# Cached attention's steps counted at every half-tile with other rates by section, and a fifth raw weight tile in the first phase of a hybrid decoder layer

## The chip, the core and the metric

The kernel runs on one core of a Trainium2 chip. The metric is the device time of one execution in microseconds (us). A core has five engines with instruction queues of their own: TensorE (PE in the profile, with its weight loads as PEld), VectorE (DVE), ScalarE (ACT), GpSimd (POOL) and SyncE (SP). Each runs its queue in order and waits on semaphores; SP, ACT and POOL also issue DMAs.

## What is computed

One layer of a decoder, for 512 prompt rows and 8 sequences of 8 sample rows, in float32:

```
h = rms_norm(x) @ w_in                       # -> q, k, v (8 heads of 128), forget gate, conv value and gate
attn  = softmax attention with cumulative log-forget bias
        prompt: 4 query blocks of 128 per head, causal
        sample: 8 queries per sequence over 2048 cached keys (16 pages of 128) and the 8 new ones
conv  = GLU -> causal depthwise conv of width 31 -> LayerNorm over channels -> swish
x = x + concat(rms_norm(attn), conv) @ w_out
x = x + relu(rms_norm(x) @ w_up)**2 @ w_down
x = x + (p @ w_ple) * sigmoid(rms_norm(x) @ w_ple_gate);   y = rms_norm(x)
```

The cache holds keys and values of 8 sequences x 16 pages x 8 heads, 128 MiB in all, fetched page by page through a page table.

## The kernel before

All 576 rows stand in the free dimension, as two halves of 288. Every float32 product is made as three matmuls on split operands: a high part (ACT copies, `whi`) and a low part (DVE subtracts, `wlo`).

**Phase 1** makes the input projection, both attentions, the convolution and the operands of the output projection. Its projection runs tile by tile: one tile is 128 output columns over 16 blocks of the contraction, cut into four chunks; `gemm_tile` (L506) yields after each half chunk. Such a *half-tile* is 12 pairs of (weight block, part) products, 24 matmuls written as L497. At each yield `half()` (L364) runs a little of the other work: steps of the convolution (`side`), of the prompt's heads (`att`), and of the cached attention (`D["dec"]`).

The weights of phase 1 come through `WStream` (L100). `high(c)` issues on ACT's queue the load of chunk c+3 into a tile `wraw`, then copies chunk c to `whi`; `low()` lets DVE subtract it to `wlo`. `get` prepares two chunks ahead. There are 4 `wraw` tiles and 3 of `whi` and `wlo` each.

The cached attention is the generator `decode` (L836): 68 steps, after a first call that only starts loads. A step n below 64 makes the scores of four pages of keys for four heads (L864); a step from 4 on makes the product of weights and values (L895) of the step four before. At every fourth step the scores' maximum is taken on DVE into the tile `dp`, and at the next the exponentials are transposed on PE (L854) through the PSUM buffer T, which the prompt's heads use as well (L749, L782, L805); ACT copies them out (L856). `kv_load` (L820) issues the loads on SP's queue: two key tiles and two value tiles for each step, each tile as two DMAs of 256 KB. Keys have 5 tiles, values 4, in two pools: `deca` (three of each, and `dp`) and `decb` (the others). A step's last call of `kv_load` comes after its matmuls, so SP waits there for the tiles that they release.

When a step runs is set by a credit: on every second half-tile `half()` adds `D["rate"]`, and at 1 it runs one step and takes 1 away. The rate comes from `DEC_RATE` by the number of the entry in `order` (L266): 11 entries (c0, q4 to c5; six convolution entries of 16 half-tiles and five others of 8), then 5 (v0, c6, k1, c7, v1), then 12 (the keys and values of heads 2 to 7). They have 136, 56 and 96 half-tiles, and are called sections 1, 2 and 3 here. In section 3 the convolution's normalisation and the prompt's heads run beside.

When the decoder is exhausted, its pools are closed and `mid` is opened for what leads to the output projection. **Phase 2** (from about 840 us) holds the output projection, MLP and gate, and is not touched.

Of the kernel before, what the change touches and what calls it, by code (L numbers as in the profile page):

```python
# [9 lines left out]
F32 = mybir.dt.float32  # L10
# [15 lines left out]
EPS = 1e-6  # L26
SCALE = 128.0 ** -0.5
NEG = -1.0e30
DEC_RATE = (11, 0.43), (16, 0.47), (99, 0.61)
DOWN_FIRST = (3, 3, 3, 4, 5, 6, 7, 8)  # L30
DOWN_PART = 7
RING = 8
# [67 lines left out]
class WStream:  # L100


    AHEAD, RAW = 2, 4

    def __init__(self, nc, pool, srcs):
        self.nc, self.pool, self.srcs = nc, pool, srcs
# [1 line left out]

    def dma(self, n):
        while self.sent < min(n, len(self.srcs)):  # L110
            t = self.pool.tile([128, 4, 128], F32, name="wraw", tag="wraw", bufs=self.RAW)
            (self.nc.sync if self.sent < self.RAW else self.nc.scalar).dma_start(t, self.srcs[self.sent])
            self.raw[self.sent] = t
            self.sent += 1
# [28 lines left out]
class Kern:  # L143
# [99 lines left out]
    def phase1(self):  # L243
# [15 lines left out]
        O_ = lambda: po_.tile([128, 512], F32, name="O", tag="O")  # L259
        D_ = lambda: pd_.tile([128, 512], F32, name="D", tag="D")  # L260
        U_ = lambda: pu.tile([128, 2, 512], F32, name="U", tag="U")
# [88 lines left out]


        side, att, fq = deque(), deque(), deque()
        D = {"credit": 0.0, "half": 0, "dec": None, "mid": None, "rate": 0.0}

        def step(q):
            while q:
                try:
                    next(q[0])
                    return True
                except StopIteration:  # L360
                    q.popleft()
            return False

        def half():  # L364

            D["half"] += 1
            odd = D["half"] % 2
            self.flush_later()
            if D["dec"] is None:
                step(att)  # L370
                step(fq)
                return
            step(side)
            step(att)
            if odd:
                return
            D["credit"] += D["rate"]
            if D["credit"] >= 1.0:
                D["credit"] -= 1.0
                if next(D["dec"], self) is self and D["mid"] is None:  # L380
                    des.close()
                    D["mid"] = mes.enter_context(tc.tile_pool(name="mid", bufs=2, reuse_waits="tile"))
                    self.ple_loads(D["mid"])
                    side.append(self.finish(1, D_, O_))

        def run(gen):
            for _ in gen:
                half()
# [41 lines left out]
        dec = D["dec"] = self.decode()  # L430
        next(dec)

        for n, (kind, i) in enumerate(order):
            D["rate"] = next(r for m, r in DEC_RATE if n < m)
            if kind == "c":
# [10 lines left out]
            if kind == "q":  # L446
                t = hd.tile([128, NR], F32, name="q", tag="q", bufs=2)
# [388 lines left out]
    def decode(self):  # L836


        nc, sm = self.nc, self.sm
        V = nc.vector.tensor_tensor  # L840
        tiles, load = self.kv, self.kv_load
        s = o = mu = p = None
        al, ls = {}, {}
        one = lambda name: sm.tile([128, 1], F32, name=name, tag=name)
        for n in range(68):
            if n == 0:
                load(0, 5)
                yield
            sc, w = n // 4, n % 4
            G, c = sc // 4, sc % 4  # L850
            if n >= 4 and w == 0:
                t = self.T_()
                for i in range(4):
                    nc.tensor.transpose(t[:, i * 128:i * 128 + 128], p[:, i * 128:i * 128 + 128], self.ident)  # L854
                for i, m in ((0, 128), (128, 512)):
                    nc.scalar.activation(self.PT[:, i:m], t[:, i:m], AF.Copy)  # L856
            if n < 64:
                if w == 0:
                    s = self.D_()
                    nc.tensor.matmul(s, self.selU[:, G, :], self.R[:, c * 512:c * 512 + 512], start=True, stop=False)  # L860
                for i in range(2):
                    kt = tiles[0][2 * n + i]
                    for h in range(4):
                        nc.tensor.matmul(s[32 * h:32 * h + 32, i * 256:i * 256 + 256].rearrange("p (a b) -> p a b", a=2),  # L864
                                         self.q_of(G // 2 * 4 + h, G % 2 * 4 + w), kt[:, :, h, :],
                                         start=False, stop=(w == 3 and i == 1))
                if w == 3:
                    p = self.kvp[0].tile([128, 512], F32, name="dp", tag="dp")
                    mx = one("dmx")
                    nc.vector.tensor_scalar(p, s, self.cns[:, G:G + 1], None, ALU.add, ALU.max, accum_out=mx)  # L870
                    new = self.mlu[:, 0, G:G + 1]
                    if c == 0:
                        nc.vector.tensor_copy(new, mx)
                        ls[sc] = self.mlu[:, 1, G:G + 1]
                    else:
                        al[sc], ls[sc] = one("dal"), one("dls")
                        V(mx, mx, new, ALU.max)
                        V(al[sc], new, mx, ALU.subtract)
                        nc.vector.tensor_copy(new, mx)
                    nm = one("dnm")  # L880
                    nc.vector.tensor_scalar(nm, mx, -1.0, None, ALU.mult)

                    def late(p=p, nm=nm, l=ls[sc], d=al.get(sc)):
                        nc.scalar.activation(p, p, AF.Exp, bias=nm, accum_out=l)
                        if d is not None:
                            nc.scalar.activation(d, d, AF.Exp)
                    self.later.append(late)
                load(0, 2 * n + 6)
            if n >= 4:
                m = n - 4  # L890
                if w == 0:
                    o = self.O_()
                for r in range(4):
                    for h in range(4):
                        nc.tensor.matmul(o[32 * h:32 * h + 32, r * 128:r * 128 + 128], self.PT[:, w * 128 + h * 32:w * 128 + h * 32 + 32],  # L895
                                         tiles[1][2 * m + r // 2][:, r % 2, h, :], start=(w == 0 and r == 0), stop=(w == 3 and r == 3))
                if w == 3:
                    self.merge(m // 16, m // 4 % 4, o, al.pop(m // 4, None), ls.pop(m // 4))
            load(1, 2 * n - 2)
            load(0, 2 * n + 7)  # L900
            yield
# [997 lines left out]
```

## Time and profile before

| | us |
|---|---|
| median of 3 runs | 2740.95 (2735.22 to 2743.04) |
| the profiled execution's own time | 2746.47 |
| span in that profile, first to last instruction | 2744.7 |
| PE busy | 2670.7 |
| DVE busy | 2043.5 |
| ACT busy | 1152.6 |
| POOL busy | 511.0 |

A span is read as PE's busy time, its idle time and what a lower granted clock adds. A view by windows gives for each stretch the busy time of each engine with the number of instructions, then the granted PE clock (1.00 is full), the mean busy share of the 16 DMA engines and the GB/s that they moved. A row of the waits has what waited, what ended the wait, us in total, times and the longest. In the timeline, `x16` counts instructions merged into one row, and a bracket gives the idle time ahead of it and what ended it; one float32 matmul of the program (L864, L895) is two of the profile.

### The profile page before, as it was taken

The page shows a single profiled execution, that of the slowest core. Times are in us where ns is not written, and L with a number is a line of the kernel's source. Part 1 is how long each engine was busy: PE and PEld are TensorE (multiplying, and loading weights), DVE is VectorE, ACT ScalarE, POOL GpSimd, SP SyncE. Part 2 cuts the span into 40 slices and gives each one's busy share as a digit, 9 for nine tenths or more (in the row PEclk, how much of TensorE's full clock was granted, in tenths as well). Part 3 has the DMA queues.
Part 4 walks back from the last instruction along what each step waited for, and adds up shares of the span by engine and source line. Part 5 has one row for each costly group of instructions (what it writes and reads, how often), then busy time and mean ns, then how long its engine had stood idle before and what let it go on. Part 6 is the DMA issues. An engine that isn't in the chain of part 4 may idle for free.

```text
span 2744.7 us, 56305 instructions
## 1 busy us (share of the span) xinstructions
PE 2670.7 (97%) x21873; PEld 2575.1 (94%) x21873; DVE 2043.5 (74%) x3553; ACT 1152.6 (42%) x1692; POOL 511.0 (19%) x906
## 2 busy tenths in 40 slices
PE   8999999998999999999999999999999999998997
PEld 8999999877889998999999999999999999998997
DVE  5577777645444447888888888898888888887676
ACT  4222232334443224444444444444444444444554
POOL 2188787601000000000000000100000000000110
PEclk9999999999999999999999999999999999999999
DMA  5488888898754454444444444666565656655675
GB/s 197 148 299 289 301 291 290 287 320 285 253 191 151 160 197 156 154 143 138 138 138 140 145 143 138 242 149 172 164 191 149 182 158 173 179 169 179 199 241 175
DMA packets 238382, 536.12 MB, mean 195 GB/s; under 512 B 25537, under 2 KB 26562, under 8 KB 238114
## 3 DMA queue, kind: packets, MB, share of 16 engines
q1 hardware_dynamic: 170978, 327.86, 37.7%
q0 software_dynamic: 33600, 143.70, 16.7%
q10 hardware_dynamic: 33536, 60.96, 6.9%
q8 instruction: 171, 2.80, 0.4%
q14 instruction: 97, 0.79, 0.1%
HBM read 441.47 MB, written 90.96 MB: 194 GB/s over the span
## 4 chain that ended last, share of the span: by engine, by line
PE 49%; issue 5%; DVE 3%; DMA 1%; ACT 1%; POOL 0%; DVEq 0%; ACTq 0%; POOLq 0%
PE P L1548 14%; PE P L1547 14%; PE P L1549 14%; PE P L1615 2%; PE P L1617 2%; PE P L1616 2%; DVE w2l L152 1%; DMA xs<-x 1%; ACT w2h L149 0%; DMA xs<-di 0%; DMA x<-c 0%; DVE w2r L1770 0%; DVE w2r L1771 0%; DVE w2r L1772 0%; DVE xs L1486 0%
## 5 line engine op out<-in xcount | busy, mean ns | idle before, releaser
L1547 PE MATMUL P<-xs,w2h 128*128 128x288 f32 x3584 | 1064.5, 297 | 17.0 <-DVE c L1664 8.0
L1548 PE MATMUL P<-xs,w2h 128*128 128x288 f32 x3584 | 1064.4, 297 | 4.7 <-DVE xs L152 4.7
L1549 PE MATMUL P<-xs,w2l 128*128 128x288 f32 x3584 | 1061.4, 296 | 2.8 <-DVE w2l L152 2.6
L149 ACT ACTIVATE w2h<-w2r 128x896 fp32r<-128x896 f32 (+1 forms) x632 | 556.0, 889 | 723.7 <-PE P L1548 425.6
L152 DVE TENSOR_TENSOR w2l<-w2r,w2h 128x896 fp32r<-128x896 f32 (+1 forms) x632 | 637.9, 1012 | 218.1 <-ACT w2h L149 215.6
L1547 PEld LDWEIGHTS P<-xs,w2h 128*128 128x128 f32 x3584 | 676.8, 189 | 23.6 <-DVE c L1664 11.1
L1548 PEld LDWEIGHTS P<-xs,w2h 128*128 128x128 f32 x3584 | 677.3, 189 | 7.3 <-DVE xs L152 7.0
L1549 PEld LDWEIGHTS P<-xs,w2l 128*128 128x128 f32 x3584 | 674.9, 188 | 5.1 <-DVE w2l L152 4.9
L497 PE MATMUL U<-xh,whi 128*128 128x288 f32 x1792 | 400.6, 305 | 3.6 <-ACT xh L149 2.2
L497 PE MATMUL U<-xh,wlo 128*128 128x288 f32 x1792 | 385.3, 297 | 1.4 <-DVE wlo L129 1.4
L497 PE MATMUL U<-xl,whi 128*128 128x288 f32 x1792 | 385.2, 297 | 1.6 <-DVE xl L331 1.6
L497 PEld LDWEIGHTS U<-xh,whi 128*128 128x128 f32 x1792 | 288.2, 190 | 22.5 <-issue 16.3
L123 ACT ACTIVATE whi<-wraw 128x512 fp32r<-128x512 f32 x224 | 141.2, 630 | 393.5 <-PE U L497 217.7
L497 PEld LDWEIGHTS U<-xl,whi 128*128 128x128 f32 x1792 | 289.8, 190 | 2.6 <-DVE xl L331 2.5
L497 PEld LDWEIGHTS U<-xh,wlo 128*128 128x128 f32 x1792 | 289.7, 190 | 2.2 <-DVE wlo L129 2.1
L129 DVE TENSOR_TENSOR wlo<-wraw,whi 128x512 fp32r<-128x512 f32 x224 | 160.2, 715 | 133.9 <-ACT whi L123 132.5
L1044 DVE SCALAR_TENSOR_TENSOR y<-ue,cv,y 128x512 f32<-128x512 f32 x240 | 183.8, 766 | 5.3
L1770 DVE TENSOR_TENSOR w2r<-w2r 128x512 f32<-128x512 f32 (+1 forms) x273 | 177.7, 651 | 5.2 <-DMA w2r<-in_w_down 5.2
L1045 POOL TENSOR_SCALAR cvt<-us,cv 128x64 f32<-128x64 f32 x240 | 162.8, 678 | 22.3
L1615 PE MATMUL P<-xs,w2h 128*128 128x288 f32 x512 | 151.8, 297 | 0.4 <-ACT c L1663 0.4
L1617 PE MATMUL P<-xs,w2l 128*128 128x288 f32 x512 | 151.0, 295 | 1.1 <-DVE w2l L152 1.0
L1616 PE MATMUL P<-xs,w2h 128*128 128x288 f32 x512 | 150.8, 295 | 0.0
(382 smaller groups left out, 2761.1 us busy)
## 6 DMA issues: line engine op xcount, KB each, us to landing
k<-in_cache_kv SPq DMA_DIRECT2D x256, 256.0 KB, 4.7
v<-in_cache_kv SPq DMA_DIRECT2D x256, 256.0 KB, 4.6
w2r<-in_w_up SPq DMA_DIRECT2D x127, 512.0 KB, 4.0
w2r<-in_w_down SPq DMA_DIRECT2D x112, 512.0 KB, 4.3
wraw<-in_w_main ACTq DMA_DIRECT2D x156, 256.0 KB, 4.9
xs<-di POOLq DMA_DIRECT2D x32, 1008.0 KB, 6.1
w2r<-in_w_gate SPq DMA_DIRECT2D x60, 512.0 KB, 4.6
x<-c POOLq DMA_DIRECT2D x48, 576.0 KB, 6.4
```

The lines of the kernel that those rows point to most:

```text
L149: self.nc.scalar.activation(out, in_, AF.Copy, **kw)
L152: self.nc.vector.tensor_tensor(out, in_, f(hi), ALU.subtract)
L497: self.nc.tensor.matmul(u[:, r, :HR], w, x[:, r * HR:(r + 1) * HR], start=first and n == 0, stop=last and n == 2)
L1044: nc.vector.scalar_tensor_tensor(y, ue[:, j:j + NPR], w, y, ALU.mult, ALU.add)
L1045: nc.gpsimd.tensor_scalar(t, us[:, :, j:j + 8], w, None, ALU.mult)
L1547: nc.tensor.matmul(o, hi[:, ia, :], s.hi[:, ib, :], start=(i == 0), stop=False)
L1548: nc.tensor.matmul(o, hi[:, ia, :], s.lo[:, ib, :], start=False, stop=False)
L1549: nc.tensor.matmul(o, lo[:, ia, :], s.hi[:, ib, :], start=False, stop=(i == n - 1))
L1615: nc.tensor.matmul(o, hi[:, ia, :], s.hi[:, kh, rows], start=first and kh == 0, stop=False)
L1616: nc.tensor.matmul(o, hi[:, ia, :], s.lo[:, kh, rows], start=False, stop=False)
L1617: nc.tensor.matmul(o, lo[:, ia, :], s.hi[:, kh, rows], start=False, stop=last and kh == 1)
L1770: lambda: V(w[:, :, 4:6, :], w[:, :, 0:1, :].broadcast_to([128, m, 2, 128]), w[:, :, 1:3, :], ALU.add),
```

## The change

Three things are changed.

1. The credit is added at every half-tile instead of every second one, and the rates are 0.2275, 0.245 and 0.2775 for each half-tile instead of 0.43, 0.47 and 0.61 for each two.
2. There are five `wraw` tiles instead of four. The first four loads still go to SP's queue and the prefetch distance stays.
3. The tile `dp` is taken from the pool `decb` instead of `deca`.

```diff
-DEC_RATE = (11, 0.43), (16, 0.47), (99, 0.61)
+DEC_RATE = (11, 0.2275), (16, 0.245), (99, 0.2775)
...
-    AHEAD, RAW = 2, 4
+    AHEAD, RAW, TILES = 2, 4, 5
...
-            t = self.pool.tile([128, 4, 128], F32, name="wraw", tag="wraw", bufs=self.RAW)
+            t = self.pool.tile([128, 4, 128], F32, name="wraw", tag="wraw", bufs=self.TILES)
...
-        D = {"credit": 0.0, "half": 0, "dec": None, "mid": None, "rate": 0.0}
+        D = {"credit": 0.0, "dec": None, "mid": None, "rate": 0.0}
...
         def half():
 
-            D["half"] += 1
-            odd = D["half"] % 2
             self.flush_later()
...
             step(side)
             step(att)
-            if odd:
-                return
             D["credit"] += D["rate"]
             if D["credit"] >= 1.0:
                 D["credit"] -= 1.0
...
-                    p = self.kvp[0].tile([128, 512], F32, name="dp", tag="dp")
+                    p = self.kvp[1].tile([128, 512], F32, name="dp", tag="dp")
```

The edits take four lines out of the file, so a line number of the changed kernel is lower by 4 from L377 on.

How far apart steps 56 to 60 stand follows from the rates. Before, they run at half-tiles 240, 244, 248, 250 and 254 of the 288; after, at 237, 241, 244, 248 and 251. Step 59 on PE: here is the way from step 58 (its L864 and L895) to it before. `xh` and `xl` are the activations' parts, numbered by block; each left-out stretch is the rest of a half-tile.

```order
L864 MATMUL D<-k,q_s 32x256 x8
L895 MATMUL O<-v,PT 32x128 x16
L497 MATMUL U<-xh_191,whi 128x288 x2
...
L757 MATMUL S<-vn,pT 128x128 x3
L497 MATMUL U<-xh_193,whi 128x288 x2
...
L864 MATMUL D<-k,q_s 32x256 x8
L895 MATMUL O<-v,PT 32x128 x16
```

And the same way after:

```order
L860 MATMUL D<-k,q_s 32x256 x8
L891 MATMUL O<-v,PT 32x128 x16
L493 MATMUL U<-xh_199,whi 128x288 x2
...
L753 MATMUL S<-vn,pT 128x128
L493 MATMUL U<-xh_201,whi 128x288 x2
...
L745 MATMUL T<-ident,p 128x128 x3
L730 MATMUL S<-cb,sel16R 128x512
...
L493 MATMUL U<-xh_203,whi 128x288 x2
...
L753 MATMUL S<-vn,pT 128x128 x2
L493 MATMUL U<-xh_205,whi 128x288 x2
...
L745 MATMUL T<-ident,p 128x128 x4
L860 MATMUL D<-k,q_s 32x256 x8
```

Between the two steps stood two half-tiles and one piece of a prompt head; now four half-tiles and four pieces stand there.

The second place is step 60 on PE, the first step of a group of four, before which the cached attention's exponentials `dp` are transposed through T. Before:

```order
L497 MATMUL U<-xh_201,wlo 128x288 x2
L805 MATMUL T<-ident,o 128x128 x4
L734 MATMUL S<-cb,sel16R 128x128
L736 MATMUL S<-maskR,identR 128x128
L737 MATMUL S<-k,q 128x128
L854 MATMUL T<-ident,dp 128x128 x4
L860 MATMUL D<-R,selU 128x512
L864 MATMUL D<-k,q_s 32x256 x8
```

After:

```order
L493 MATMUL U<-xh_195,wlo 128x288 x2
L753 MATMUL S<-vn,pT 128x128 x4
L850 MATMUL T<-ident,dp 128x128 x4
L856 MATMUL D<-R,selU 128x512
L860 MATMUL D<-k,q_s 32x256 x8
```

Before, a prompt head's transposes (L805) stood in the same half-tile and took T first; now the half-tile has a head's product with its values in S, and T is taken once.

## The prediction

> **What bounds the kernel now.** I start with the first row of the page and ask where TensorE (PE) is not busy.
>
> ```profile
> PE 2670.7 (97%) x21873; PEld 2575.1 (94%) x21873; DVE 2043.5 (74%) x3553; ACT 1152.6 (42%) x1692; POOL 511.0 (19%) x906
> ```
>
> PE is busy for 2670.7 of 2744.7 us, so everything that a better order can win is in the 74 us of idle time and in what a lower clock costs. The change touches only the first phase, from the first cached-attention step (about 106 us) to the last (765 us). I cut that phase into stretches that nearly match the three rate sections of the code and the drain behind them. The columns are busy time by engine, then the granted PE clock, the DMA share and GB/s.
>
> ```profile
> 140.00:383.00 243.00, 242.95 (x2637) 224.14 (x2635) 187.19 (x315) 62.39 (x109) 190.70 (x344) 1.00 0.88 295
> 383.00:507.00 124.00, 123.19 (x1348) 112.73 (x1347) 93.32 (x174) 36.12 (x74) 94.38 (x168) 1.00 0.89 295
> 507.00:744.00 237.00, 219.14 (x2336) 188.87 (x2334) 124.57 (x354) 97.36 (x234) 44.40 (x88) 0.96 0.86 287
> 744.00:870.00 126.00, 121.76 (x950) 109.66 (x950) 58.57 (x151) 50.69 (x111) 7.39 (x15) 0.99 0.54 182
> ```
>
> Sections 1 and 2 keep PE busy to within 0.9 us, with DMA at 295 GB/s. Section 3 loses 17.9 us of PE and some clock. What PE waits for there, by the waits from 540 to 740 us:
>
> ```profile
> PE O L895 <- DMA v<-in_cache_kv: 11.4, 13, 2.1
> PE T L854 <- ACT amt L807: 2.9, 1, 2.9
> PE O L895 <- ACT yl L1090: 1.1, 1, 1.1
> ```
>
> So 11.4 us is cached values that have not landed, in 13 waits. The stretch around 680 us shows what such a wait looks like; the bracket at the end of a row is the idle time before it.
>
> ```profile
> 674.85 1.07 PE L864 MATMUL D<-k,q_s 128*32 128x256 f32 x16
> ...
> 681.45 1.07 PE L864 MATMUL D<-k,q_s 128*32 128x256 f32 x16
> 683.49 0.43 PE L895 MATMUL O<-v,PT 128*32 128x128 f32 x8 [0.97 <-DMA v<-in_cache_kv]
> 684.96 0.66 PE L895 MATMUL O<-v,PT 128*32 128x128 f32 x8 [1.04 <-DMA v<-in_cache_kv]
> 686.34 0.65 PE L895 MATMUL O<-v,PT 128*32 128x128 f32 x8 [0.72 <-DMA v<-in_cache_kv]
> 688.26 0.66 PE L895 MATMUL O<-v,PT 128*32 128x128 f32 x8 [1.27 <-DMA v<-in_cache_kv]
> 688.85 0.85 PE L497 MATMUL U<-xh,whi 128*128 128x288 f32 x2
> ```
>
> Two steps begin 6.6 us apart (674.85 and 681.45); the second waits four times, 4.0 us, and the projection behind it runs at half clock (two matmuls take 0.85 instead of 0.42). That loss shows in short windows too:
>
> ```profile
> 440.00:460.00 20.00, 19.19 (x210) 17.51 (x209) 17.83 (x37) 6.67 (x14) 17.64 (x31) 1.00 0.92 303
> 460.00:480.00 20.00, 20.00 (x217) 18.59 (x216) 15.26 (x22) 3.40 (x7) 17.45 (x29) 1.00 0.91 305
> 480.00:500.00 20.00, 20.00 (x217) 18.50 (x216) 15.84 (x29) 6.59 (x12) 14.61 (x27) 1.00 0.95 309
> 600.00:620.00 20.00, 16.98 (x132) 13.90 (x131) 6.51 (x14) 6.36 (x16) 1.08 (x2) 0.83 0.92 306
> 680.00:700.00 20.00, 14.48 (x124) 11.91 (x122) 9.56 (x31) 6.72 (x14) 1.49 (x3) 0.83 0.92 312
> 700.00:720.00 20.00, 18.67 (x252) 16.21 (x253) 8.28 (x25) 10.77 (x22) 2.69 (x5) 0.91 0.84 277
> ```
>
> Work lost to the clock is busy time times the missing share: 16.98 x 0.17 + 14.48 x 0.17 + 18.67 x 0.09 = 2.9 + 2.5 + 1.7 = **7.1 us**. At stake in section 3: 11.4 + 2.9 + 1.1 + 7.1 = **22.5 us**. (The other 2.5 us of idle time there are short waits on DVE and ACT that the change does not address.)
>
> The Trainium skill bears on the clock term: TensorE: Matmul & The Clock Gate, section "Why this matters for your kernels", asks for no PE-idle gap over about 3 us, since a whole idle window halves the clock. The longest single gap in the rows above is 2.9 us, so by that rule the clock term would be 0 and 15.4 us would be at stake. The rows decide against so strict a reading: several gaps of about 1 us in a row already came with a 0.83 clock.
>
> **The change part by part. The counting and the rates.** A half-tile adds 0.43/2 = 0.215, 0.235 and 0.305 of a step by section before, and 0.2275, 0.245 and 0.2775 after. Sections 1 and 2 have 136 and 56 half-tiles. When section 3 begins, 136 x 0.215 + 56 x 0.235 = 42.4 steps are credited before, and 30.94 + 13.72 = 44.7 after: 2.26 steps leave section 3. Both versions credit the 69th step, which ends the decoder, at half-tile 280, so what opens behind it stays in place, and the total of decoder steps, matmuls and DMAs is unchanged. A step costs PE 1.9 us:
>
> ```profile
> 633.27 1.07 PE L864 MATMUL D<-k,q_s 128*32 128x256 f32 x16
> 634.16 1.06 PE L895 MATMUL O<-v,PT 128*32 128x128 f32 x32
> 635.15 0.40 PE L497 MATMUL U<-xh,whi 128*128 128x288 f32 x1
> ```
>
> That PE work moves 4.3 us from section 3 into sections 1 and 2 and cancels in the sum. What does not cancel is DMA demand. Each step issues 8 loads of 256 KB on SP's queue, 2.10 MB. Answers for the DMAs from 140 to 383 us, and from 507 to 744 us:
>
> ```profile
> DMA packets 38718, 71.64 MB, mean 295 GB/s; under 512 B 4551, under 2 KB 4615, under 8 KB 38683
> ...
> v<-in_cache_kv SPq DMA_DIRECT2D x100, 256.0 KB, 4.6
> k<-in_cache_kv SPq DMA_DIRECT2D x98, 256.0 KB, 4.9
> ```
>
> ```profile
> DMA packets 34245, 67.97 MB, mean 287 GB/s; under 512 B 4591, under 2 KB 4591, under 8 KB 34214
> ```
>
> What each section would need if PE never waited:
> - Section 3 before: 67.97 MB in 237 - 22.5 = 214.5 us, 317 GB/s. It got 287 and stalled. After: 67.97 - 2.26 x 2.10 = 63.2 MB in 214.5 - 4.3 = 210.2 us, **301 GB/s**.
> - Section 1 after: its 198 loads (51.9 MB) grow by 0.2275/0.215, 5.8%: 74.7 MB in 243 + 1.45 x 1.9 = 245.8 us, **304 GB/s** (295 before).
> - Section 2 after: 295 x 124 = 36.6 MB plus 0.56 step, 37.8 MB in 125.1 us, **302 GB/s**.
>
> So the change makes three unequal demands equal. Can about 303 GB/s flow without a wait? The three windows from 440 to 500 us say yes for 60 us: 303, 305 and 309 GB/s with 0.8 us of PE idle, none of it for a cached tile. At 0.91 to 0.95 they leave little above that.
>
> **The spacing.** Steps now fall only on even half-tiles; in section 3 they are 4, 4 and 2 half-tiles apart. The two-half-tile pairs are where it hurts, since v has four tiles, two for each step, and a step's loads go out when the step two before it releases them. After, the distances are 4 and 3 (4 and 5 in section 1 instead of 4 and 6), so the 6.6 us pair above becomes about 9 us for the same 2.1 MB. Steps can also fall on odd half-tiles. The 2.9 us wait belongs here: at that step the transposes of the new head's output (L805) and of the cached attention (L854) share the one T buffer in one half-tile; after, only the latter stands there.
>
> **The fifth raw tile.** ACT issues the load of chunk c+3 ahead of its own copy of chunk c. With four tiles the load takes the tile that DVE's subtraction of chunk c-1 still reads; with five, that of c-2. The rows around the 2.9 us wait, for ACT, DVE, SP and PE:
>
> ```profile
> 697.36 0.34 ACTq L112 DMA_DIRECT2D wraw<-in_w_main  x1
> 698.08 0.63 ACT L123 ACTIVATE whi<-wraw 128x512 fp32r<-128x512 f32 x1 [4.50 <-PE T L805]
> ...
> 700.61 0.67 ACT L807 ACTIVATE amt<-T,gat 128x512 f32<-128x512 f32 x1
> ```
>
> ```profile
> 696.60 0.69 DVE L129 TENSOR_TENSOR wlo<-wraw,whi 128x512 fp32r<-128x512 f32 x1
> ```
>
> ```profile
> 694.31 8.60 SPq L832 DMA_DIRECT2D v<-in_cache_kv  x4
> ```
>
> ```profile
> 701.33 0.67 PE L854 MATMUL T<-ident,dp 128*128 128x128 f32 x4 [2.85 <-ACT amt L807]
> ```
>
> ACT's load goes out at 697.36, just after DVE's subtraction ends at 697.29, with ACT idle for 4.5 us; amt, behind it in ACT's queue, is what PE waits for. SP's four value loads take 8.6 us to issue meanwhile. In totals, ACT's waits for wlo from 150 to 520 us, then SP's waits for weight landings from 520 to 740:
>
> ```profile
> ACT whi L123 <- DVE wlo L129: 35.2, 15, 4.7
> ```
>
> ```profile
> SPq L832 <- DMA wraw<-in_w_main: 56.2, 17, 7.7
> ```
>
> The 35.2 us lie under a PE that is 100% busy, so there they are worth 0. If that cover were gone, they would cost at most 35.2. In section 3 an earlier weight load releases SP's queue earlier. I put no separate gain on it beyond the 22.5, and no loss below 0: no load is added. Moving dp to the other pool changes no instruction; 0.
>
> **The sum.** Of 22.5 us the floor is 0 and the ceiling 22.5. Steps that come right behind a two-half-tile distance lose about two thirds of the 11.4 us; the rest is backlog that a demand of 301 instead of 317 should mostly clear. I leave 4 us of waits and 2 us of clock: gain 22.5 - 6 = 16.5 us. The profiled execution took 2746.47 us, so it would take 2730.0; it lay 5.5 above the median of 2740.95, on which the same gain gives **2724.5 us**.
>
> **The rivals.**
> - *Everything goes.* If DMA has ample room, no wait is left: 2740.95 - 22.5 = 2718.5. For it: 312 GB/s at a 0.92 share in the worst window. Against: that window stalls. DMA: Bandwidth & Descriptors of the Trainium skill, section "Bandwidth", points this way: about 358 GB/s for a core that shares its memory, 425 alone. No window above comes near that.
> - *DMA's limit is just above what sections 1 and 2 draw.* All three stretches carry 71.64 + 36.6 + 67.97 = 176.2 MB in 604 us. At 297 GB/s that takes 593 us: 11 us less, of which 3 to 10 would be left beside PE's own waits, 2731 to 2738. For it: spreading cannot help a queue that is full everywhere. Against: the 60 us at 306.
> - *Slower: the stall spreads.* If a queue held at 0.9 yields only the 287 GB/s of section 3, sections 1 and 2, now asking 302 to 304, run out of their lead: 176.2/287 = 614 us, 10 us more, 2751. It decides below 176.2/604 = 292 GB/s. Against: 295 flows there today with PE never waiting.
> - *It does nothing.* Waits move to other steps and keep their sum: about 2741.
>
> **How the numbers follow.** Chances: forecast 0.55 (2717 to 2731 by itself), everything goes 0.15, DMA limit 0.17, slower 0.07, nothing 0.06. The range reaches from 2714, the ceiling with 0.15% for the run, to 2746, where it leaves out the slower case and little else. A measurement tells about 0.3% from no change, 8.2 us, so faster means below 2732.7: the first two cases and a little of the third, 0.74; the same 0.18; slower 0.08.
>
> **What would show it.** Right: the waits of the cached-values matmuls for v between 540 and 740 us fall from 11.4 to under 4, no 20 us window there has a clock of 0.83, the wait for amt is gone, section 3's DMA falls near 300 GB/s with sections 1 and 2 rising to 302 to 304, and PE stays 100% busy in section 1. Wrong: v waits before 500 us, or as many in section 3 at lower GB/s, which would mean that order in the queues and not bytes sets the pace. The fifth tile is right if ACT's waits for wlo shrink by most of 35.2.

## The result, and the profile after

The changed kernel takes 2726.55 us (median of 19 runs, 2718.74 to 2734.1) against 2743.04 before (19 runs): a ratio of 0.9941, interval 0.9931 to 0.9952, or 16.2 us less (13.2 to 18.9). Measured once more beside the later experiments it had 0.9949 (0.9933 to 0.9965).

A profile shows one execution, and that can lie several us off its kernel's median. The first profile of the changed kernel took 2718.74 us, the fastest of its runs; the second, 2727.41, lies near its median, so sizes are taken from that one. The profile of before (2746.47) lies 3 us above the median that it is compared with here, and 7 to 11 above before's medians beside the experiments (2735.3 to 2738.9), so what is read against it comes out somewhat large. Of the kernels below, the profiles of "five tiles, old counting, new rates" and "changed, more steps early" lie 10 and 7 us above their own medians, the others within 4.3. One of the ten executions of "before, few values loaded" took 7408 us and is left out of its ratio.

The page's first row after, and the three sections by windows in the first profile, cut where the projection's tiles 21 and 28 begin (374 and 505 us; before these begin at 376 and 503, and the prediction cut at 383 and 507). The fourth row is section 3 in the second profile:

```profile
PE 2658.2 (98%) x21873; PEld 2566.3 (94%) x21873; DVE 2042.8 (75%) x3553; ACT 1149.9 (42%) x1692; POOL 511.5 (19%) x906
```

```profile
140.00:374.00 234.00, 233.89 (x2566) 214.74 (x2565) 176.03 (x297) 58.65 (x102) 189.37 (x334) 1.00 0.89 296
374.00:505.00 131.00, 128.72 (x1416) 116.52 (x1415) 97.77 (x189) 39.44 (x80) 91.15 (x168) 1.00 0.89 298
505.00:720.00 215.00, 208.31 (x2278) 184.90 (x2277) 126.54 (x345) 95.00 (x226) 46.47 (x90) 1.00 0.90 306
504.00:725.00 221.00, 212.34 (x2293) 188.19 (x2293) 125.82 (x344) 96.00 (x233) 47.74 (x92) 0.99 0.88 300
```

Section 3 has a clock of 1.00 and 0.99 in the two profiles instead of 0.96, and moves 306 and 300 GB/s instead of 287. Section 2, which hardly waited before, now has 2.3 us of PE idle time (1.7 in the second profile). The waits of PE from 505 to 720 us in the first profile, then those from 370 to 520:

```profile
PE T L745 <- ACT p L739: 1.2, 2, 0.7
PE T L850 <- ACT amt L803: 1.0, 1, 1.0
PE O L891 <- DMA v<-in_cache_kv: 1.0, 3, 0.5
```

```profile
PE O L891 <- DMA v<-in_cache_kv: 2.2, 3, 1.2
PE T L850 <- ACT v_s L779: 0.7, 1, 0.7
```

In section 3 value waits fell from 11.4 to 1.0 us (1.8 in the second profile), and the wait for `amt` from 2.9 to 1.0. In section 2, value waits appeared that were not there before (2.2 and 1.5 us). ACT's waits for `wlo` from 150 to 520 us (35.2 before) have no row any more; its copies to `whi` wait longer for PE instead (142.1 us, 108.3 before) and for the weights' own landing (5.3 before):

```profile
ACT whi L123 <- DMA wraw<-in_w_main: 20.2, 7, 4.8
```

To see where time went, I take from each trace when the first projection matmul of tiles 2, 4, 21, 28 and 40 starts. (A tile has 96 of them, so a half-tile has 12, six pairs, and not the 24 that the description of the kernel gives.) "Start" runs up to tile 2; section 3 includes the drain up to the output projection. All in us of the profiled execution; the ratio is of timed runs. In every kernel but before, "before, few values loaded" and "four tiles, old counting, new rates", `dp` is in the other pool.

| kernel | start | section 1 | section 2 | section 3 | ratio to before, interval |
|---|---|---|---|---|---|
| before | 40.5 | 280.2 | 126.8 | 331.2 | 1 |
| changed, first profile | 35.4 | 282.7 | 131.0 | 307.1 | 0.9941 (0.9931 to 0.9952) |
| changed, second profile | 35.5 | 283.0 | 130.7 | 310.7 | 0.9949 (0.9933 to 0.9965) |
| four tiles, new counting, new rates | 39.2 | 283.0 | 136.5 | 308.4 | 0.9997 (0.9973 to 1.002) |
| five tiles, old counting, old rates | 35.6 | 280.0 | 125.8 | 321.8 | 0.9963 (0.9944 to 0.9982) |
| four tiles, old counting, new rates | 38.8 | 285.7 | 136.5 | 321.0 | 1.0026 (1.0005 to 1.0048) |
| four tiles, new counting, old rates | 38.7 | 282.1 | 126.6 | 320.9 | 0.9995 (0.9975 to 1.0015) |
| five tiles, new counting, old rates | 35.8 | 279.9 | 126.5 | 323.8 | 0.9986 (0.9969 to 1.0003) |
| five tiles, old counting, new rates | 35.2 | 286.7 | 137.0 | 311.3 | 0.9972 (0.9958 to 0.9986) |
| changed, fewer steps early | 35.2 | 281.9 | 127.3 | 324.5 | 0.998 (0.9964 to 0.9997) |
| changed, more steps early | 35.7 | 299.8 | 142.6 | 301.8 | 1.0014 (0.9995 to 1.0032) |
| changed, fifth tile at the start only | 37.4 | 283.6 | 138.8 | 308.6 | 0.9987 (0.9971 to 1.0003) |
| before, few values loaded | 39.6 | 280.2 | 125.8 | 307.2 | 0.9942 (0.9921 to 0.9963) |
| changed, few values loaded | 35.8 | 283.7 | 127.8 | 303.2 | 0.9919 (0.989 to 0.9948) |

From before to the second profile: start -5.0, section 1 +2.8, section 2 +3.9, section 3 -20.5. Part of this is only steps that moved. Counted by their score matmuls, the sections have 29, 13 and 22 steps before and 30, 14 and 20 after: one whole step more in each of the first two and two fewer in the third (the prediction had 1.70, 0.56 and 2.26), 1.9 us each. In waits and clock that leaves -5.0 at the start, +0.9 in section 1, **+2.0 in section 2** and **-16.7 in section 3**. These add up to 18.8, more than the 16.2 of the timed runs, as the profile of before lies above its medians.

The 5.0 at the start, too, is somewhat large. In before's profile, PE has a low clock from 35 to 40 us, worth about 1.4 us of its work (4.07 x 0.34):

```profile
35.00:40.00 5.00, 4.07 (x19) 4.00 (x19) 2.95 (x4) 1.86 (x3) 0.00 (x0) 0.66 0.01 3
```

The three other kernels with four tiles and all loads have a clock of 1.00 there and a start of 38.7 to 39.2 us, against 35.2 to 35.8 with five tiles for all chunks. So the tile is worth 3 to 4 us at the start.

### The profile page after: what moved, and what is told of

Read it like the earlier page. It is cut to its first block, busy times and chain, and to the rows that moved or that the text cites. A ratio compares the mean times of both kernels' runs of the same rounds, so it can differ in the third digit from the quotient of the medians.

```text
span 2717.0 us, 56291 instructions
## 1 busy us (share of the span) xinstructions
PE 2658.2 (98%) x21873; PEld 2566.3 (94%) x21873; DVE 2042.8 (75%) x3553; ACT 1149.9 (42%) x1692; POOL 511.5 (19%) x906
## 4 chain that ended last, share of the span: by engine, by line
PE 54%; DVE 4%; issue 1%; ACT 1%; DMA 1%; DVEq 0%; ACTq 0%; POOLq 0%
PE P L1543 15%; PE P L1544 15%; PE P L1545 15%; PE P L1611 2%; PE P L1613 2%; PE P L1612 2%; DVE w2l L152 1%; ACT w2h L149 0%; DMA xs<-x 0%; DVE xs L152 0%; DMA x<-c 0%; DVE w2r L1766 0%; DVE w2r L1767 0%; DVE c L1675 0%; DVE c L1660 0%
## 5 line engine op out<-in xcount | busy, mean ns | idle before, releaser
L1543 PE MATMUL P<-xs,w2h 128*128 128x288 f32 x3584 | 1065.7, 297 | 16.2 <-DVE c L1660 8.7
```

The lines of the kernel that those rows point to most:

```text
L1543: nc.tensor.matmul(o, hi[:, ia, :], s.hi[:, ib, :], start=(i == 0), stop=False)
```

## The experiments

**Which part does it: the tile, the counting or the rates?** Four kernels undo or take one or two of the three.

Four raw tiles again, everything else as changed (the edit is against the changed kernel):

```diff
-    AHEAD, RAW, TILES = 2, 4, 5
+    AHEAD, RAW, TILES = 2, 4, 4
```

> The change with four raw weight tiles again; counting, rates and the place of dp as changed. Three theories share out the 16.5 us. DEMAND: what counts is how many MB each section asks of the DMA engines, so the rates. SPACING: what counts is that no two cached steps stand two half-tiles apart. QUEUE: what counts is that ACT's weight load no longer waits for DVE, since SP's loads wait for weight landings. DEMAND and SPACING both expect the whole gain here, 14 to 18 us below before, and ACT's waits for wlo from 150 to 520 us back near 35 us. QUEUE expects at most half of the gain, 5 to 9 us below before, with value waits of 6 us or more in section 3.

Measured: 0.9997 (0.9973 to 1.002), nothing is left of the gain. DEMAND and SPACING fall as theories of the whole. QUEUE expected up to half of the gain to stay, and 6 us or more of value waits in section 3, where there are 2.7. Section 3 keeps its short time (308.4), but section 2 is 9.7 us longer than before and the start 3.8 us longer than with five tiles. (1.9 us of the 9.7, here and in the other kernels with 14 steps in section 2, are the step that moved.) In section 2 (here 379 to 516 us) the clock is 0.98 and DMA moves less than before:

```profile
379.00:516.00 137.00, 132.36 (x1420) 120.17 (x1419) 96.67 (x188) 39.55 (x80) 93.82 (x167) 0.98 0.88 285
```

PE's waits there from 370 to 520 us, and below them what SP's loads wait for from 150 to 520 us in this kernel, then in the changed one:

```profile
PE O L891 <- DMA v<-in_cache_kv: 4.9, 5, 1.8
```

```profile
SPq L828 <- DMA wraw<-in_w_main: 85.8, 50, 4.8
```

```profile
SPq L828 <- DMA wraw<-in_w_main: 66.4, 42, 3.6
```

With four tiles SP spends 19 us more on waiting for weights to land (as the profile attributes its waits), around the stretch in which values come late. The total alone does not decide: before, also with four tiles, had 67.6, and the fewer early steps below have 86.2 with five.

The fifth tile alone (against the kernel before; `dp` is moved too):

```diff
-    AHEAD, RAW = 2, 4
+    AHEAD, RAW, TILES = 2, 4, 5
...
-            t = self.pool.tile([128, 4, 128], F32, name="wraw", tag="wraw", bufs=self.RAW)
+            t = self.pool.tile([128, 4, 128], F32, name="wraw", tag="wraw", bufs=self.TILES)
```

> Before with the fifth raw tile alone (and dp in the other pool); old counting and old rates. DEMAND and SPACING: no change within 3 us, the 11.4 us of value waits in section 3 stay between 9 and 13. QUEUE: 6 to 12 us below before, value waits under 7.

Measured: 0.9963, 10 us below before, as QUEUE said. A third to a half of that is the start; value waits fall, though not under the 7 us that QUEUE gave, and the wait for `amt` in T stays (waits of PE from 495 to 760 us):

```profile
PE O L895 <- DMA v<-in_cache_kv: 7.5, 7, 1.9
PE T L854 <- ACT amt L807: 3.6, 1, 3.6
```

The new rates alone (against the kernel before):

```diff
-DEC_RATE = (11, 0.43), (16, 0.47), (99, 0.61)
+DEC_RATE = (11, 0.455), (16, 0.49), (99, 0.555)
```

> Before with the new rates alone, counted at every second half-tile as 0.455, 0.49 and 0.555; four raw tiles. Section 3 now asks for about 301 GB/s, but its steps stand 4, 4, 4, 4 and 2 half-tiles apart, so some pairs at two half-tiles stay. DEMAND: 12 to 17 us below before. SPACING: the share of such pairs falls from one in three to one in five, so a third of the gain or so, 3 to 8 us.

Measured: 1.0026, slower than before. Both theories missed the sign. Section 3 gains 10.2 us, and sections 2 and 1 lose 9.7 and 5.5.

The new counting alone, old rates halved (against the changed kernel):

```diff
-DEC_RATE = (11, 0.2275), (16, 0.245), (99, 0.2775)
+DEC_RATE = (11, 0.215), (16, 0.235), (99, 0.305)
...
-    AHEAD, RAW, TILES = 2, 4, 5
+    AHEAD, RAW, TILES = 2, 4, 4
```

> Counting at every half-tile with the old rates, 0.215, 0.235 and 0.305, and four raw tiles. Section 3 asks for 317 GB/s as before, but its steps stand 3 or 4 half-tiles apart. DEMAND: 0 to 5 us below before, value waits in section 3 of 8 us or more. SPACING: 11 to 17 us below before, value waits under 5.

Measured: 0.9995, no difference, which fits DEMAND in time; but value waits were 4.0 us, below what DEMAND expected. Other waits took their place (waits of PE from 100 to 860 us):

```profile
PE O L891 <- DMA v<-in_cache_kv: 4.0, 4, 1.5
PE O L891 <- ACT PT L852: 4.0, 3, 3.0
PE T L745 <- ACT p L739: 3.5, 1, 3.5
```

**What does the fifth tile set free?** The same two, with five tiles. First the counting with the old rates (against the changed kernel):

```diff
-DEC_RATE = (11, 0.2275), (16, 0.245), (99, 0.2775)
+DEC_RATE = (11, 0.215), (16, 0.235), (99, 0.305)
```

> Counting at every half-tile with the old rates, five raw tiles. With four tiles this counting was worth nothing (ratio 0.9995), and the fifth tile alone 10 us. QUEUE, in its new form: the fifth tile takes ACT's waits for DVE out of SP's way, and only then can even spacing or other rates help. If spacing is what the tile sets free, this is within 4 us of the changed kernel (0.992 to 0.9955 of before); if it is the rates, this stays at the fifth tile's own 0.9963.

Measured: 0.9986 (0.9969 to 1.0003). Not within 4 us of the changed kernel; if anything above the fifth tile's own 0.9963, though the intervals overlap. So spacing without the rates is not it. Then the new rates counted at every second half-tile (against the kernel before; `dp` is moved too):

```diff
-DEC_RATE = (11, 0.43), (16, 0.47), (99, 0.61)
+DEC_RATE = (11, 0.455), (16, 0.49), (99, 0.555)
...
-    AHEAD, RAW = 2, 4
+    AHEAD, RAW, TILES = 2, 4, 5
```

> The new rates counted at every second half-tile, five raw tiles. With four tiles these rates made it 0.26% slower, since section 2 then stalled (9.7 us longer) as much as section 3 gained (10.2 us shorter). If the rates are what the fifth tile sets free: within 4 us of the changed kernel, section 2 at most 5 us longer than before. If spacing: 0.9963 or a little above, section 2 still 8 us or more longer.

Measured: 0.9972, section 2 at 137.0 us, near what was expected if spacing is what the tile sets free. Section 3 gains 20 us, as in the changed kernel, but section 2 still loses 10:

```profile
378.00:515.00 137.00, 131.27 (x1417) 117.64 (x1416) 97.56 (x189) 39.60 (x81) 91.70 (x167) 0.99 0.84 279
```

So the rates shorten section 3, and what keeps section 2 from paying for it needs both others: with these rates, only even spacing and the fifth tile together have it at 131 (two profiles) and not at 136.5 to 139 (one profile of each of four kernels). This profile was the slowest execution of its kernel, so its 137.0 alone proves little; the timed ratio, 6 to 9 us above the changed kernel, points the same way.

**Where is DMA's limit?** Fewer and more steps early, around the changed rates (against the changed kernel, both):

```diff
-DEC_RATE = (11, 0.2275), (16, 0.245), (99, 0.2775)
+DEC_RATE = (11, 0.2225), (16, 0.24), (99, 0.2875)
```

> The changed kernel with rates 0.2225, 0.24 and 0.2875. In the changed kernel value waits now stand in section 2 (1.2, 0.7 and 0.3 us), which is 4.2 us longer than before, and section 3 has a lead of 5 us. If DMA's limit lies just under the 302 GB/s asked of section 2, this wins 1 to 5 us on the changed kernel: 0.992 to 0.994 of before. If the limit is not reached there, no difference, 0.994 to 0.995.

Measured: 0.998, 8 to 11 us above the changed kernel, where 1 to 5 less were hoped for. Section 2 came down to 127.3 as expected (it has 13 steps again, as many as before), and that with SP waiting 86.2 us for weights from 150 to 520 us, as much as with four tiles; but section 3 rose to 324.5. One step left it instead of two, so it asks for (67.97 - 2.10) MB in 212.6 us, 310 GB/s, and gets 291 at a 0.97 clock:

```profile
500.00:735.00 235.00, 220.69 (x2354) 193.57 (x2353) 131.58 (x369) 101.37 (x240) 48.15 (x95) 0.97 0.86 291
```

```diff
-DEC_RATE = (11, 0.2275), (16, 0.245), (99, 0.2775)
+DEC_RATE = (11, 0.245), (16, 0.26), (99, 0.245)
```

> The changed kernel with rates 0.245, 0.26 and 0.245: sections 1 and 2 would ask for 316 and 312 GB/s, section 3 for about 280. This looks for DMA's limit. At 300 GB/s the 118 MB of sections 1 and 2 take 394 us, some 12 us longer than PE needs; so 8 to 14 us above the changed kernel (0.997 to 1.000 of before), with 6 us or more of value waits before 505 us. If 316 GB/s can flow, as in the worst window of before (312), there are no more than 3 us of waits there and the time is that of the changed kernel.

Measured: 1.0014, a little above the range given for a limit near 300: 15.3 us of value waits before 534 us, sections 1 and 2 longer by 19.6 and 15.8 us (8 and 2 of it are four steps and one that moved in). Asked for 316 and 312 GB/s by their rates, they got 296 and 284:

```profile
140.00:392.00 252.00, 243.88 (x2720) 219.85 (x2713) 180.06 (x311) 60.23 (x107) 186.45 (x336) 1.00 0.88 296
392.00:534.00 142.00, 133.48 (x1412) 117.68 (x1411) 94.68 (x177) 37.24 (x76) 90.32 (x167) 0.98 0.85 284
```

So in these patterns of steps 303 GB/s asked of section 3 (two steps fewer than before) flowed and 310 did not, and in no kernel did sections 1 and 2 get more than 298. It is not shown that the rate itself is the limit, since the steps also fall beside other work in each pattern. It is no ceiling of the DMA engines either: in section 3 of the changed kernel they moved far more over 40 us, with PE busy throughout (and before, from 660 to 680 us, 351 GB/s):

```profile
660.00:680.00 20.00, 20.00 (x217) 17.98 (x217) 14.55 (x42) 12.99 (x30) 3.90 (x8) 1.00 1.01 365
680.00:700.00 20.00, 20.00 (x280) 18.79 (x279) 12.21 (x37) 10.71 (x20) 2.72 (x6) 1.00 1.04 382
```

**A control, the start, and the ceiling.** The changed kernel again:

> The changed kernel once more, beside the other kernels of this set, since the single edits were measured on other chips than it. Every theory: 0.993 to 0.995 of before, as measured first. If the last profile of the changed kernel was a lucky one, section 3 is here more than 5 us longer than the 307 us that it took there.

Measured: 0.9949, section 3 at 310.7 us. It holds; the first profile was 3.6 us shorter there.

Against the changed kernel, only the fifth load of the program has a tile of its own, behind it a ring of four:

```diff
-            t = self.pool.tile([128, 4, 128], F32, name="wraw", tag="wraw", bufs=self.TILES)
+            w5 = self.sent == self.RAW
+            t = self.pool.tile([128, 4, 128], F32, name="wraw", tag="wraw5" if w5 else "wraw", bufs=1 if w5 else self.RAW)
```

> The changed kernel with a ring of four raw tiles, of which only the fifth load of the program has a tile of its own; from the tenth load on ACT waits for DVE's subtraction of the chunk before, as before. The six profiles so far show the first two projection tiles at 35.4 to 35.8 us with five tiles and 38.7 to 40.5 with four. If the start is one part of the fifth tile's gain and the loads in sections 2 and 3 the other: start at 35 to 37 us, section 2 at 135 us or more, 0.997 to 0.999 of before. If the start were all, 0.993 to 0.995.

Measured: 0.9987, start at 37.4 (about half of its gain; a little above the 35 to 37 expected), section 2 at 138.8. So the start is one part and the later loads the other, the larger. ACT's waits for `wlo` from 150 to 520 us are back:

```profile
ACT whi L124 <- DVE wlo L130: 39.7, 17, 6.8
```

And no loads of values beyond the first four tiles, in the kernel before and in the changed one, so that later steps multiply old values:

```diff
             n = len(self.kv[i])
+            if i == 1 and n >= 4:
+                self.kv[i].append(self.kv[i][n % 4])
+                continue
```

> Before without the loads of cached values beyond the first four tiles: the later steps use those four again, so about 40% of the DMA bytes of the three sections are left out, and no step waits for values. All theories put the 22.5 us at stake down to late values and to what follows from them, so 18 to 26 us below before (0.9905 to 0.9935), with the start still at 39 to 40 us. If it gains less than 12 us, the waits would only have moved to something else that bounds section 3.

Measured: 0.9942 (0.9921 to 0.9963), 16 us less, 2 us short of what was expected (the interval, 10 to 22 us, takes 18 in). No step waits for values, and section 3 takes 307.2 us with DMA at 203 GB/s:

```profile
501.00:720.00 219.00, 213.91 (x2375) 189.45 (x2363) 128.25 (x360) 97.62 (x234) 47.94 (x94) 1.00 0.62 203
```

So the loads of values cost before about 16 us in the timed runs, by coming late and by what follows from it. Leaving them out also takes their traffic away from all other loads, and no run tells the two apart. The 22.5 read from the profile include what that profile was above the median.

> The changed kernel without the loads of cached values beyond the first four tiles. If the change works through late values and through the start alone, this stands 3 to 6 us under the kernel before with the same loads left out (the start's gain), and 5 to 10 us under the changed kernel. If even spacing helps for another reason, such as the T buffer, the distance between the two is 8 us or more.

Measured: 0.9919 (0.989 to 0.9948). That is 6 us under the kernel before with the same loads left out by the ratios, 8.6 by the medians. On four runs that does not decide between the start alone (3 to 6) and a further gain of even spacing (8 or more). It is 8 us under the changed kernel (0.9949 to 0.9919, intervals that overlap). So the changed kernel seems to leave some 8 us to the loads of values.

## Why the prediction was right, and where it was not

The number held: 16.5 us were forecast, 16.2 measured. That the two agree so closely is luck, as the steps show one by one:

- *Section 3's waits are late values and what follows.* Right. Leaving out the loads (few values) takes section 3 from 331 to 307 us, and the changed kernel, with two steps fewer there, reaches 307 to 311. Between the profiles its waits and clock shrank by 16.7 us. The timed gain leaves about 14 to 16 for it: 16.2, plus 2.9 lost in sections 1 and 2, less 3 to 5 at the start (an estimate from these rows). The forecast had 16.5 of 22.5.
- *22.5 us at stake.* Somewhat large. The timed ceiling was 16 us (10 to 22); the profiled execution of before was slower than most.
- *The rates make three demands equal, and 303 GB/s can flow without a wait, as 60 us at 306 show.* **This step failed for section 2.** With the rates it lost about 10 us (four tiles, or even-only steps) and 3.9 in the changed kernel, 2.0 of it waits. The sum had it too small to begin with: a whole step went into section 2 and not 0.56, which is 38.7 MB in 125.9 us, 307 GB/s and not 302. It got 298, and 60 good microseconds before did not carry over to it. Section 1 moved 296 where 304 was forecast: by its end 8 cache loads more had gone out than before (234 against 226), and all 8 of them before 140 us. But bytes alone do not set the pace: the kernels with four tiles or even-only steps have the same 14 steps in section 2, got 279 to 285 GB/s there and stalled. The rival "the stall spreads" foresaw such stalls and was given 0.07. Its reason, that the queue yields only 287 GB/s, does not fit, since section 3 got 300 and 306.
- *The fifth raw tile: no gain beyond the 22.5.* **This was the step that failed most.** Alone it is worth 10 us, and without it the rest is worth nothing. I had read its 35.2 us of ACT waits as lying under a busy PE, and did not look at the start. There ACT's first two weight loads (the fifth and sixth of the program) stand ahead of its copies of x, and wait for DVE. ACT before, from 8 us on:

```profile
8.18 0.39 ACTq L112 DMA_DIRECT2D wraw<-in_w_main  x1
8.62 0.63 ACT L123 ACTIVATE whi<-wraw 128x512 fp32r<-128x512 f32 x1 [0.66 <-DVE wlo L129]
10.01 0.34 ACTq L112 DMA_DIRECT2D wraw<-in_w_main  x1
10.39 0.63 ACT L123 ACTIVATE whi<-wraw 128x512 fp32r<-128x512 f32 x1 [1.14 <-DVE wlo L129]
10.93 1.43 ACT L149 ACTIVATE xh<-xraw,vecs 128x576 fp32r<-128x576 f32 x2
```

and after:

```profile
7.92 0.62 ACT L123 ACTIVATE whi<-wraw 128x512 fp32r<-128x512 f32 x1
8.08 0.34 ACTq L112 DMA_DIRECT2D wraw<-in_w_main  x1
9.35 0.63 ACT L123 ACTIVATE whi<-wraw 128x512 fp32r<-128x512 f32 x1 [0.82 <-DMA wraw<-in_w_main]
9.89 1.43 ACT L149 ACTIVATE xh<-xraw,vecs 128x576 fp32r<-128x576 f32 x2
```

  The split of x on which PE waits (`xh`, then `xl`) begins 1.0 us sooner. Over the first 42 us ACT waits 3.9 us for `wlo` before and not at all after. PE's waits for the split fall from 3.8 us to 1.0 (before, then after):

```profile
ACT whi L123 <- DVE wlo L129: 3.9, 3, 2.1
PE U L497 <- ACT xh L149: 2.2, 3, 1.2
PE U L497 <- DVE xl L331: 1.6, 3, 0.9
```

```profile
PE U L493 <- DVE xl L331: 1.0, 3, 0.4
```

  That the tile acts in section 2 is shown: 136.5 and 138.8 us without it there, 131 with it, with the same steps. So it was not worth 0 under a busy PE. The way is not settled. One guess is that the weight load goes out late and SP's loads of keys and values wait for it to land. For it: from 150 to 520 us those waits are 85.8 and 86.5 us without the tile, 66.4 with it. Against it: fewer early steps have 86.2 with five tiles and a section 2 of 127.3 us. From 520 to 740 us they fell from 56.2 to 38.6 us (the row below), but that goes with the rates and not with the tile: it is 41.3 with the other changes and four tiles, 52.3 with the fifth tile alone.

```profile
SPq L828 <- DMA wraw<-in_w_main: 38.6, 17, 4.9
```

- *Even spacing.* Right only in company. With the old rates it gave nothing (0.9995 with four tiles, 0.9986 with five); with the new ones and five tiles section 2 is at 131 instead of 137 us (0.9972 against 0.9941 to 0.9949).
- *The T buffer.* Right in part: 2.9 us became 1.0, at an earlier step.
- *The clock.* Right: it is 1.00 in all three sections of the first profile after, and 0.99 in section 3 of the second. Behind them, up to 802.5 us, PE waits 2.5 us, and the stretch around has

```profile
796.00:806.00 10.00, 7.53 (x33) 5.70 (x32) 5.70 (x16) 4.28 (x9) 0.67 (x2) 0.86 0.79 295
```

  The Trainium skill's TensorE: Matmul & The Clock Gate ("Why this matters for your kernels") allows gaps up to about 3 us; here, as before, a gap under that came with a lower clock (0.50 from 804 to 806 us).
- *The signs.* Value waits from 540 to 740 us fell under 4, no 20 us window there had a clock of 0.83 (the lowest was 0.91, in the second profile), and ACT's waits for `wlo` are gone. PE stayed busy in section 1. But sections 1 and 2 rose only to 296 and 298 GB/s, not to 302 to 304, and one sign of being wrong came: value waits before 500 us, 1.5 us of them (1.3 in the second profile).

So the forecast landed on the sum because terms it did not have cancelled against a section 3 gain read somewhat too large: 3 to 5 us won at the start, 2.9 lost in sections 1 and 2.

What stays open, beside the tile's way in section 2, is why single patterns do badly. The counting at every half-tile with old rates has new waits for `p` and `PT` of 3.5 and 4 us with four tiles and with five; fewer steps early has 3.3 for `amt` and 3.1 for `PT`. These probably come from which steps fall beside which piece of a prompt head; I have not separated that from the demand for bytes. Moving `dp` was not measured alone.

## What to carry to other kernels

Do not put a wait at nothing because it lies under a busy engine, least of all when the waiting queue also issues DMAs: here the fifth tile behind the start was worth about 8 us (0.9987 against 0.9949, less 1.9 at the start). And look at the start of the program, where nothing is covered. When work that brings its own traffic is moved into a stretch that runs at nine tenths of the DMA engines, count in whole steps what that stretch will ask for, and look at what it sustains over its whole length, not in its best windows. And measure the parts of a change together as well as apart: here two parts were worth nothing or less until the third was there.

## Not expected of the hardware

A fifth buffer for 256 KB loads on ACT's queue made other loads, on SP's queue, come less late. With the same steps in section 2, PE waited 4.9 and 6.4 us for values from 370 to 520 us without it there, and 2.2 and 1.5 with it. The lower DMA rate of the slower kernels, 279 to 285 GB/s against 298, is no finding of its own: the bytes are nearly the same (298 x 131 and 285 x 137 are both 39 MB), so it says once more that the section took longer. A waiting PE delays ACT, and with it the next weight load, which may keep such a stall going; no run tells that apart. Between 303 and 310 GB/s asked of section 3 lay 14 us of its time, 2 of them the step that stayed.
